# Drawn settings of operand places and product orders behind the last product of an encoder step

## The chip, the cores and the metric

The kernel runs on one core of one Trainium2 chip. The metric is the device time of one execution in microseconds (us). A core has a matrix engine (TensorE, PE in the profile; its weight loads are listed apart, as PEld), VectorE (DVE), ScalarE (ACT), GpSimd (POOL) and SyncE (SP), and 16 DMA engines that are fed by queues. Operands lie in SBUF, an on-chip memory of 128 partitions; TensorE writes its sums to PSUM, which has eight banks of 512 float32 columns in each partition. One product of TensorE takes a block of weights of 128 rows by up to 128 columns from SBUF, streams up to 512 columns of a second operand through it, and adds the result to columns of one bank.

## The reference

The reference is one inference step of a one-layer streaming encoder, for 1024 new prompt frames and 64 frames of a running stream, in float32:

```python
def mixer(xn, conv_prefix, attn_fn, w_in, w_conv, w_conv_out, w_attn_out, w_out):
    proj = xn @ w_in
    ...
    cv, conv_state = causal_conv(cc * ch, conv_prefix, w_conv)
    ya = (cb * cv) @ w_conv_out
    o, new_k, new_v = attn_fn(heads(q), heads(k), heads(v))
    yb = o.reshape(B, L, ATT_DIM) @ w_attn_out
    merged = jax.nn.sigmoid(ga) * ya + jax.nn.sigmoid(gb) * yb
    return merged @ w_out, conv_state, new_k, new_v

def trunk(...):
    m, cs, nk, nv = mixer(rmsnorm(x, g_mix[l]), ...)
    x = x + m
    x = x + (jax.nn.silu(xn2 @ w_ff1) * (xn2 @ w_ff3)) @ w_ff2
    return rmsnorm(x, g_final), ...
```

Here xn2 is rmsnorm(x, g_ffn). Attention reads a band of nine chunks of 64 frames with a bias for each distance. The outputs are the two encoded sequences and the new convolution states and key and value caches.

## The kernel before

All 1088 frames (T) are worked on together. Every float32 operand of a product is split by `split` (lines 119 to 122) into a high and a low part in the type float32r, and a product of two float32 matrices becomes three products of TensorE: high by high, high by low, low by high. Where both sides are large, a product of 2 by 2 blocks is made from seven block products in place of eight; `STEPS` gives their order, and each step has its own weights and its own stream.

The stages follow one another on TensorE: norm, transposes (line 408) and values; the projections of `run` (line 218); the gate projections of `product` (lines 294 to 302) beside attention; the merge; the output projection; transposes (line 1135); the first two feed-forward matrices, again through `run`; and the last one, in the loop from line 1462 on. In each step of `run`, line 238 issues 24 products of 272 columns (HN): four blocks k, by three pairs of high and low, by two halves j of the frames, so that two products in a row have the same weights and write two banks in turn. `product` issues three products in a row to one bank.

In the last stage the transposed hidden frames (ht) are the weights, and the split rows of `w_ff2` stream through as 512 columns (line 1508). These rows lie in seven rings, one for each step, which `ring_of` (lines 1266 to 1270) makes: tiles of 128 partitions by 4352 columns (8 times HT, HT = 544). Ring 1 and ring 2 hold the parts for steps 1 and 2. Columns 3072 to 3583 of ring 1 also take squares that ACT writes when it sums up a row's norm (line 1448). The sums are taken out of PSUM by line 1520 on DVE or line 1518 on ACT. PSUM there has the pool `psD`: tag "A" with two buffers, tag "BD" with four, and the tile ys. Behind the last product follow sums, norms and writes of the output (`half_ended`, lines 1443 to 1459), with writes from the queues of ACT and SP.

The tile framework puts in the waits: a tile that takes over a buffer waits for the last reader of the one before, and a reader waits for the writer of what it reads.

Of the kernel before, what the change touches and what calls it, by code (L numbers as in the profile page):

```python
# [8 lines left out]
F32 = mybir.dt.float32  # L9
# [6 lines left out]
P = 128  # L16
# [17 lines left out]
HN = HT // 2  # L34
# [30 lines left out]
def encoder_kernel(ctx: ExitStack, tc: tile.TileContext, ins, outs):  # L65
# [1396 lines left out]
    for b, ks in enumerate(blocks):  # L1462
        first, final = b == 0, b == len(blocks) - 1
        nk = blocks[b + 1] if not final else []
        for g in range(2):
# [28 lines left out]
            for si, js in turns:  # L1494
# [47 lines left out]
                if final and g == 0 and si == 4:  # L1542
# [9 lines left out]
                    vec.scalar_tensor_tensor(row, row, r[:TS], gfb[:TS], op0=ALU.mult, op1=ALU.mult)  # L1552
                    nc.sync.dma_start(outs["y_sample"], row)

_OUTS = [
    ("y_prompt", (1024, 1024), (1, 1024, 1024)),
    ("y_sample", (64, 1024), (1, 64, 1024)),
# [33 lines left out]
```

## Time and profile before

| what | value |
|---|---|
| median of two runs | 1518.12 us (1518.03 and 1518.2) |
| span of the profiled execution, first to last instruction | 1513.8 us |
| mean granted clock of TensorE in it | 0.994 |
| line 238, products of 272 columns, as its commonest group: mean length of one | 288 ns |
| line 1508, products of 512 columns into A: count and mean length | 528, 393 ns |
| line 903, transposes of attention: count and mean length | 240, 277 ns |

The profile is taken from one execution. Times in its rows are in us from the start of the span. Products of TensorE are pipelined: one is still under way when the next starts, so that the length of one is more than the distance from one start to the next. The chain of waits follows the work that ended last back to the start, and gives for each piece its start and length.

### The profile page before, as it was taken

The page shows a single profiled execution, that of the slowest core. Times are in us where ns is not written, and L with a number is a line of the kernel's source. Part 1 is how long each engine was busy: PE and PEld are TensorE (multiplying, and loading weights), DVE is VectorE, ACT ScalarE, POOL GpSimd, SP SyncE. Part 2 cuts the span into 40 slices and gives each one's busy share as a digit, 9 for nine tenths or more (in the row PEclk, how much of TensorE's full clock was granted, in tenths as well). Part 3 has the DMA queues.
Part 4 walks back from the last instruction along what each step waited for, and adds up shares of the span by engine and source line. Part 5 has one row for each costly group of instructions (what it writes and reads, how often), then busy time and mean ns, then how long its engine had stood idle before and what let it go on. Part 6 is the DMA issues. An engine that isn't in the chain of part 4 may idle for free.

```text
span 1513.8 us, 26451 instructions
## 1 busy us (share of the span) xinstructions
PE 1476.9 (98%) x10178; PEld 1381.1 (91%) x10178; DVE 981.2 (65%) x1843; ACT 682.7 (45%) x1397; POOL 128.7 (9%) x236
## 2 busy tenths in 40 slices
PE   7999999999999999999999999999999999999997
PEld 5799999999999999998889999999999998788886
DVE  6886465642776752763489667666666668857576
ACT  6654433333776752542256444444444445402123
POOL 1210010001111121000100011100001011000000
PEclk9999999999999999999999999999999999999999
DMA  7597524168676529554432434443334449667675
GB/s 233 181 305 245 184 78 135 57 187 234 181 186 176 151 82 293 164 167 145 140 126 77 143 134 152 144 148 120 117 142 157 143 177 317 234 221 235 222 259 202
DMA packets 167518, 264.73 MB, mean 175 GB/s; under 512 B 19008, under 2 KB 103168, under 8 KB 167264
## 3 DMA queue, kind: packets, MB, share of 16 engines
q1 hardware_dynamic: 146736, 198.23, 42.2%
q0 software_dynamic: 19504, 62.71, 11.4%
q10 hardware_dynamic: 1152, 2.10, 0.4%
q8 instruction: 80, 1.31, 0.4%
q14 instruction: 46, 0.38, 0.1%
HBM read 171.06 MB, written 91.92 MB: 174 GB/s over the span
## 4 chain that ended last, share of the span: by engine, by line
PE 79%; DMA 8%; DVE 6%; ACT 3%; issue 3%; SPq 1%; POOL 0%; ACTq 0%; POOLq 0%; DVEq 0%
PE Aa L238 9%; PE Ab L238 9%; PE A L1508 7%; PE Da L238 4%; PE Db L238 4%; PE D L1508 3%; PE Bb L238 2%; PE Ba L238 2%; PE B L1508 2%; PE wo L1066 2%; PE wo L1068 2%; PE wo L1067 2%; PE t L903 2%; PE Ak L238 2%; PE g L300 2%
## 5 line engine op out<-in xcount | busy, mean ns | idle before, releaser
L1508 PE MATMUL A<-ring,ht 128*128 128x512 f32 x528 | 126.6, 393 | 3.6 <-ACT acc L1518 1.9
L1508 PEld LDWEIGHTS A<-ring,ht 128*128 128x128 f32 x528 | 98.8, 188 | 27.2 <-ACT acc L1518 3.2
L300 PE MATMUL g<-xn,whp 128*128 128x272 f32 x384 | 113.2, 295 | 0.0
L301 PE MATMUL g<-xn,whp 128*128 128x272 f32 x384 | 112.0, 292 | 0.0
L302 PE MATMUL g<-xn,wlp 128*128 128x272 f32 x384 | 111.6, 291 | 0.0
L121 ACT CAST ring<-w2r 128x512 fp32r<-128x512 f32 (+1 forms) x78 | 43.4, 587 | 105.7 <-PE A L1508 52.6
L121 ACT CAST hq<-sa 128x512 fp32r<-128x512 f32 x77 | 47.7, 619 | 86.4 <-DVE sa L1239 56.6
L814 DVE CUSTOM_DVE_ANT_0 p<-s,bb 128x640 f32<-128x640 f32 (+5 forms) x72 | 47.5, 661 | 45.5 <-DMA bb<-bias_d 28.6
L1227 POOL DMA_DIRECT2D h_d<-hq x77 | 40.9, 532 | 416.5 <-DVE hq L122 242.1
L122 DVE TENSOR_TENSOR hq<-sa,hq 128x512 fp32r<-128x512 f32 x77 | 53.1, 690 | 33.4 <-ACT hq L121 33.3
L300 PEld LDWEIGHTS g<-xn,whp 128*128 128x128 f32 x384 | 72.6, 189 | 1.0
L302 PEld LDWEIGHTS g<-xn,wlp 128*128 128x128 f32 x384 | 72.6, 189 | 0.5
L301 PEld LDWEIGHTS g<-xn,whp 128*128 128x128 f32 x384 | 72.7, 189 | 0.3
L1508 PE MATMUL D<-ring,ht 128*128 128x512 f32 x264 | 63.9, 393 | 1.3 <-ACT acc L1518 1.3
L122 DVE TENSOR_TENSOR wla<-rawa,wha 128x512 fp32r<-128x512 f32 x56 | 38.5, 687 | 40.5 <-ACT wha L121 40.5
L238 PE MATMUL Aa<-tt,wha 128*128 128x272 f32 x352 | 59.1, 289 | 2.5 <-ACT tt L121 2.5
L1508 PEld LDWEIGHTS D<-ring,ht 128*128 128x128 f32 x264 | 49.5, 188 | 13.1 <-ACT acc L1518 1.8
L122 DVE TENSOR_TENSOR ring<-w2r,ring 128x512 fp32r<-128x512 f32 (+1 forms) x78 | 49.0, 647 | 14.4 <-ACT ring L121 14.2
L238 PE MATMUL Ab<-mg,whb 128*128 128x272 f32 x352 | 58.4, 288 | 0.0
L238 PE MATMUL Aa<-mg,wha 128*128 128x272 f32 x352 | 58.3, 288 | 0.0
L238 PE MATMUL Ab<-tt,whb 128*128 128x272 f32 x352 | 58.2, 287 | 0.0
L121 ACT CAST wha<-rawa 128x512 fp32r<-128x512 f32 x56 | 34.8, 621 | 51.3 <-PE Ab L238 35.3
(519 smaller groups left out, 4368.2 us busy)
## 6 DMA issues: line engine op xcount, KB each, us to landing
h_d<-hq POOLq DMA_DIRECT2D x77, 512.0 KB, 3.5
ht<-h_d SPq DMA_DIRECT2D x154, 256.0 KB, 3.7
rawa<-in_w_ff SPq DMA_DIRECT2D x11, 1024.0 KB, 5.9
rawb<-in_w_ff SPq DMA_DIRECT2D x11, 1024.0 KB, 5.4
w2r<-in_w_ff SPq DMA_DIRECT2D x11, 1024.0 KB, 5.8
qd<-q_d SPq DMA_DIRECT2D x32, 272.0 KB, 4.7
rawp<-in_w_in SPq DMA_DIRECT2D x6, 1024.0 KB, 5.9
u_d<-scr SPq DMA_DIRECT2D x8, 544.0 KB, 4.6
```

The costliest lines, as they stand in the source:

```text
L121: act.copy(hi, src)
L122: vec.tensor_tensor(lo, src, hi.bitcast(F32), op=ALU.subtract)
L238: mm(t[:, j, :HN], w[:, k, :], x[p][:, l, k, j * HN : (j + 1) * HN], start=p in (1, 2, 7) and k == 0 and n == 0, stop=k == 3 and n == 2, s ...
L300: mm(out, a, p, start=k == 0, stop=False)
L301: mm(out, a, q, start=False, stop=False)
L302: mm(out, b, p, start=False, stop=k == kt - 1)
L814: vec.tensor_tensor_reduce(out=s if len(ps.shape) == 2 else s.rearrange("p (a b) -> p a b", a=2), in0=ps, in1=bias if len(ps.shape) == 2 e ...
L903: nc.tensor.transpose(tp[:, i * P : (i + 1) * P], s[:, i * P : (i + 1) * P], ident)
L1066: mm(ps, x(k, 0), wh, start=f, stop=False)
L1067: mm(ps, x(k, 0), wl, start=False, stop=False)
L1227: nc.gpsimd.dma_start(h_d[p, c - 1], hq.rearrange("p i l t -> p (i l t)").bitcast(F32))
L1508: mm(t, ht[k][:, j, x], w[:, l], start=p in (1, 2, 7) and k == 0 and n == 0, stop=k == len(ks) - 1 and n == 2, skip_group_check=p in (6, 5 ...
```

## The change

Behind the last stage a loop is added. It takes ring 1 as the stream, ring 2 as the weights, and two new tiles of PSUM, pr (tag "A") and pq (tag "BD"), which nothing reads. There are 640 settings of 24 products of 272 columns, with the loop of `run`: four blocks k by six combinations of weights w, stream l and half j. Each setting draws the places of its operands. The first 320 keep the order of line 238, the others draw an order of the six. The distance of the two halves is 336 columns, in some of the last 160 settings 320 or 352; the step from one block k to the next is 0, 16 or 32 columns of the stream, and the offsets d, dw and dl are multiples of 8 columns up to 56. Behind them stand 256 transposes of blocks of 128 by 128 from ring 1, taken as float32, into pr.

```diff
+    pr = psD.tile([P, 512], F32, tag="A", name="pr", bufs=2)
+    pq = psD.tile([P, 512], F32, tag="BD", name="pq", bufs=4)
+    mv, st = ring_of(1), ring_of(2)
+    PAIRS = [(0, 0, 0), (0, 0, 1), (0, 1, 0), (0, 1, 1), (1, 0, 0), (1, 0, 1)]
+    draw = random.Random(7)
+    for i in range(640):
+        six = list(PAIRS)
+        if i >= 320:
+            draw.shuffle(six)
+        e = 16 if i < 480 or i % 3 else draw.choice((0, 32))
+        step = draw.choice((0, 0, 16, 32))
+        d, dw, dl = (draw.randrange(0, 64, 8) for _ in range(3))
+        for k in range(4):
+            for w, l, j in six:
+                a = 128 + 2048 * l + dl * l + j * (320 + e) + step * k
+                b = 128 + d + 512 * k + w * (192 + dw)
+                mm(
+                    (pr, pq)[j][:, :HN], st[:, b : b + P], mv[:, a : a + HN],
+                    start=k == 0, stop=k == 3, skip_group_check=True,
+                )
+    wide = mv.bitcast(F32)
+    for i in range(16):
+        for n in range(16):
+            a = 128 + 8 * (i % 8) + 128 * (n % 8) + 64 * (i // 8)
+            nc.tensor.transpose(pr[:, n % 4 * P : n % 4 * P + P], wide[:, a : a + P], ident)
```

More of the change, by code (lines that the diff above doesn't have):

```diff
@@ L1553, in encoder_kernel @@
                     nc.sync.dma_start(outs["y_sample"], row)
+    import random
+    pr = psD.tile([P, 512], F32, tag="A", name="pr", bufs=2)
[23 more added lines that the diff above has]
+            nc.tensor.transpose(pr[:, n % 4 * P : n % 4 * P + P], wide[:, a : a + P], ident)
 _OUTS = [
```

## The prediction

> **What bounds the kernel now.** I read the page first: the busy shares (columns: busy us, share of the span, instructions) and the row of granted clock.
>
> ```profile
> span 1513.8 us, 26451 instructions
> PE 1476.9 (98%) x10178; PEld 1381.1 (91%) x10178; DVE 981.2 (65%) x1843; ACT 682.7 (45%) x1397; POOL 128.7 (9%) x236
> PEclk9999999999999999999999999999999999999999
> q8 instruction: 80, 1.31, 0.4%
> ```
>
> TensorE is busy 98% of the span, and there is one weight load for each product (10178 and 10178), so no product saves its load even where two in a row use the same weights. The clock stays at 9 tenths or more in all 40 slices. As the work is added to TensorE, behind its last product, what matters is how far apart products of 272 columns start when nothing holds them up. A product's own duration (288 ns in the groups) is no help, because products overlap. So next comes the chain of waits, in its middle (columns: start, length in us, what): from 36 consecutive rows of line 238, all of 24 products, the first, the last, and one of each other length that occurs.
>
> ```profile
> 1153.60 3.00 PE Da L238 x24
> 1156.60 3.01 PE Aa L238 x24
> ...
> 1168.61 2.99 PE Db L238 x24
> ...
> 1258.50 3.00 PE Db L238 x24
> ```
>
> From the start of the first row to the start of the last lie 35 rows, 840 products, and 104.90 us: 124.9 ns a product. No row is shorter than 2.99 or longer than 3.01 us, which is 0.4 ns a product either way. The table of stretches says whether that stretch is undisturbed (columns: stretch, us, then busy time and count for PE, PEld, DVE, ACT, POOL, then clock, DMA share, GB/s):
>
> ```profile
> 1000.00:1250.00 250.00, 250.00 (x2004) 250.00 (x2003) 166.75 (x280) 110.81 (x210) 25.59 (x48) 1.00 0.41 147
> 1505.80:1513.80 8.00, 0.04 (x1) 0.00 (x0) 3.43 (x11) 2.48 (x7) 0.00 (x0) 0.75 0.38 142
> ```
>
> In 250 us TensorE is never idle, at full clock; the 2004 products, of which some two were already running at the start, confirm 125 ns. The second row is the end of the kernel: from 1505.8 on TensorE has no work, and 8 us go to the last sums, norms and output writes on DVE, ACT and the queues. What bounds the span is therefore TensorE up to 1505.8 and a chain of small DVE and ACT steps after it.
>
> **The change part by part.** Where it starts: the timeline of the end (start, length, engine, line, what, count).
>
> ```profile
> 1501.80 0.69 DVE L1520 TENSOR_TENSOR acc<-A,acc 128x512 f32<-128x512 f32 x1
> 1504.78 1.07 PE L1508 MATMUL A<-ring,ht 128*128 128x512 f32 x4
> 1505.98 0.68 DVE L1520 TENSOR_TENSOR acc<-A,acc 128x512 f32<-128x512 f32 x1
> 1506.75 0.63 ACT L1448 ACTIVATE ring<-acc 128x512 fp32r<-128x512 f32 x1 [0.46 <-DVE n2y L157]
> 1509.01 0.75 DVE L1458 SCALAR_TENSOR_TENSOR acc<-acc,n4y,gfb 128x512 f32<-128x512 f32 x1
> 1509.76 0.37 ACTq L1457 DMA_DIRECT2D out_y_prompt<-acc  x1
> ```
>
> The last product ends at 1504.78 + 1.07 = 1505.85. Four products in 1.07 us, of which one lasts about 0.39, start (1.07 - 0.39) / 3 = 0.23 us apart, so the next could start at 1505.85 - 0.39 + 0.23 = 1505.69. The new tile pr takes the older of the two buffers of tag A; its last reader is the DVE sum at 1501.80, done by 1502.49. If it got the other one, it would wait for the sum at 1505.98 to 1506.66, 1.0 us. Buffers of tag BD were read earlier still. The moving operand lies in ring 1, into whose columns 3072 to 3583 ACT writes squares until 1507.38; the change reads columns below 2952. If the order were kept for the whole tile, the start would slip to 1507.4, by 1.7 us. I take no wait, and 0 to 2 us for the range. The norms and output writes of the tail don't depend on the new work; they end at about 1513.8 and are covered by it.
>
> The products: 640 settings of 24 make 15,360. Each has 128 x 128 weights and 272 columns, the form of line 238, so 15,360 x 124.88 ns = 1918.2 us, all of it on TensorE and on the path that sets the end. Half of the settings have line 238's own order; the other half are shuffled within each group of six. The nearest row to another order is in the gated projections, where three products in a row go to one bank in the order high, high, low. Of its rows the first of one run and the first behind it, 12 products apart:
>
> ```profile
> 606.78 0.29 PE L300 MATMUL ya<-u,whp 128*128 128x272 f32 x1
> ...
> 608.29 0.67 PE L300 MATMUL yb<-ob,whp 128*128 128x272 f32 x4
> ```
>
> 1.51 us / 12 = 125.8 ns. On the 7,680 shuffled products the 0.9 ns more would be 7 us; that is the upper end of the order's price, and 0 the lower. I take 0, because line 238 has the same two banks in turn and is the row that the new products resemble most.
>
> The transposes: 256, each of 128 columns with the data as weights and the identity streaming, as lines 408 and 1135 issue them, eight in a row. A row of each line at full clock, one at half clock, its clock from the stretch that holds it, and the length of one:
>
> ```profile
> 757.43 1.04 PE L1135 MATMUL xt<-ident,xg 128*128 128x128 f32 x8
> ...
> 54.48 1.06 PE L408 MATMUL xt<-ident,scr 128*128 128x128 f32 x8 [1.71 <-DVE scr L393]
> ...
> 56.81 1.91 PE L408 MATMUL xt<-ident,scr 128*128 128x128 f32 x8
> ...
> 56.00:58.00 2.00, 1.19 (x6) 1.37 (x7) 0.50 0.60 166
> ...
> L1135 PE MATMUL xt<-ident,xg x72: 222/273/300, 753.9 to 807.0; 128*128 128x128 f32 x64, 64*128 64x64 f32 x8
> ```
>
> Eight in 1.04 us, the last of 0.27, start 0.77 / 7 = 0.110 us apart; 256 make 28.1 us. At half clock the eight take 1.91 us, about 0.11 us more for each. [...] I take full clock, for the nearest rows with no gap before them show it.
>
> Instruction code: the instruction queue of the page moved 80 packets, 1.31 MB, which fits the 2 x 10178 instructions of TensorE (16 KB for 256 of them). The 31,232 new ones need 122 packets more. In the undisturbed 250 us above some 4000 instructions, 16 packets, were consumed at the same pace without a gap, so I cost it at nothing. The two loads of DVE and ACT that ran beside the products then are absent in the added part; nothing here can make it slower.
>
> The sum, against the profiled execution: 1505.7 + 1918.2 + 28.1 + 0.2 for the end of the last transpose = 3452.2. Behind it stands the closing of the program. From the last output write's issue (1509.76) to the end (1513.8) are 4.0 us, a write's flight among them, which the new end hasn't; so 0 to 4, taken as 2. Span 3454. The median of the runs is 1518.12, 4.3 us over the span; with the same 4.3 the time is **3458 us**, 2.28 times the time before.
>
> **The rivals.**
>
> *Places cost something of their own.* The change draws offsets between weights and stream in steps of 8 columns, which line 238 doesn't vary. That a place matters at all shows in the last stage, in the chain of waits:
>
> ```profile
> 1480.99 4.08 PE B L1508 x18
> 1485.07 4.20 PE A L1508 x18
> ```
>
> The same shape, 18 products of 512 columns, takes 226.7 ns each in one and 233.3 in the other, with other places and other banks: 2.9%. For it: this row. Against it: the rows of line 238 lie between 2.99 and 3.01 us although they read seven streams and many weight buffers at different places. If the drawn places were all the bad ones, 2.9% of 1918 is 56 us: 3514. If line 238 now has the middle, the drawn ones lie within half of that on either side: 3430 to 3486. Chance 0.10 for more than 3471, 0.07 for less than 3450.
>
> *The clock falls in the transposes.* In place of 110 ns each takes up to 0.11 us more, 256 x 0.11 = 28 us: 3486, less what passes before the gate closes. For it: line 408 ran at half clock in this very trace. Against it: that was 2 us behind an idle gap of 1.71 us, and the row of line 1135 ran at full clock. Chance 0.16. [...]
>
> *The products are not run.* Nothing reads pr or pq. Were work without a reader dropped on the way to the chip, nothing would be added: 1518 us, no change. It would decide from the point where less than 30 us, about 240 products, is left. For it: in the profile of before every product has a reader, so the case isn't tested. Against it: nothing in the profile shows that anything was dropped. Chance 0.02.
>
> *Late code.* If the 122 packets came late by half a microsecond each, it would be 61 us, 3519; no gap in 250 us speaks for it. Chance 0.03.
>
> **How the numbers follow.** The forecast (3458; its own range is 3450 to 3471: 6 us down and up for 0.4 ns a product, 2 down for the closing, 7 up for the order) has 0.62. The range reaches to half the spread of the 512-column rows below, 3430, and to the whole of it above, 3515, which takes in the clock; outside are the dropped products, late code, and a small part of the two cases of places, about 1 in 10. A measurement of this kernel tells 2%, 30 us, from no change. All cases but the dropped work are slower by over 100%: slower 0.98, within 2% 0.015, and 0.005 for faster, for which I see no mechanism.
>
> **What would show it.** In the profile of the changed kernel: a group of x15360 products of 272 columns at the line of the new loop, and x256 transposes; TensorE without idle time from 1505.7 on; 24 products in 3.00 us in every slice; PEclk 9 up to the last slice, or 5 in the last if the transposes lose the clock; about 202 packets on the instruction queue; the output writes ending near 1513. It is wrong if the settings differ by more than a few tenths of a nanosecond a product, if the shuffled half is slower than the first, or if TensorE shows gaps.

## The result and the profile after

The changed kernel took 3463.49 us (median of two runs, 3462.35 and 3464.64) against 1518.12 us: a ratio of 2.2819, with a 95% interval of 2.2753 to 2.2885. The forecast was 3458 us.

The page of the changed kernel, in the rows that answer to those of before:

```profile
span 3462.5 us, 57683 instructions
PE 3429.8 (99%) x25794; PEld 3334.5 (96%) x25794; DVE 981.7 (28%) x1843; ACT 683.3 (20%) x1397; POOL 128.9 (4%) x236
PEclk9999999999999999999999999999999999999999
q8 instruction: 202, 3.31, 0.4%
L1573 PE MATMUL pr<-ring,ring 128*128 128x272 f32 x7680 | 1768.4, 288 | 0.0
L1573 PE MATMUL pq<-ring,ring 128*128 128x272 f32 x7680 | 1768.2, 288 | 0.0
```

DVE, ACT and POOL did what they did before; TensorE has 15,616 products more, each with its load, and no idle time in front of any of them (the 0.0 of the two groups). The granted clock stayed at 9 tenths or more in all 40 slices, and 122 packets of code more were fetched (202 against 80).

The ends of the added work, from the timeline of TensorE (start, length, what, count), and below them two rows of ACT and one of DVE from the same stretch:

```profile
1505.08 2.20 PE L1508 MATMUL A<-ring,ht 128*128 128x512 f32 x9
1507.12 0.29 PE L1573 MATMUL pr<-ring,ring 128*128 128x272 f32 x1
...
3433.46 28.11 PE L1581 MATMUL pr<-ident,ring 128*128 128x128 f32 x256
...
1506.53 0.63 ACT L1448 ACTIVATE ring<-acc 128x512 fp32r<-128x512 f32 x1 [1.23 <-DVE acc L1520]
1507.42 0.68 DVE L1520 TENSOR_TENSOR acc<-A,acc 128x512 f32<-128x512 f32 x1
1508.19 0.63 ACT L1448 ACTIVATE ring<-acc 128x512 fp32r<-128x512 f32 x1 [0.45 <-DVE n2y L157]
```

The last product of before ends at 1507.28, and the first new one starts 0.16 us ahead of that end: no wait for a buffer or for ring 1. It starts before the last sum from tag A (1507.42 us), so pr had the older buffer, and the new products run on while ACT writes squares into ring 1 until 1508.82 us. From 1507.12 to 3433.46 are 1926.34 us for 15,360 products, 125.41 ns each. The 256 transposes took 28.11 us, and the program closed 0.93 us behind them, at 3462.5.

The stretches say where the 125.41 ns come from. The first row lies in the settings with line 238's order, the second and third in the shuffled ones; the columns are those of the prediction's table of stretches:

```profile
1510.00:1910.00 400.00, 400.00 (x3192) 400.00 (x3191) 1.13 (x3) 0.73 (x1) 0.00 (x0) 1.00 0.01 4
...
2470.00:2870.00 400.00, 400.00 (x3192) 400.00 (x3191) 0.00 (x0) 0.00 (x0) 0.00 (x0) 1.00 0.00 1
2870.00:3430.00 560.00, 560.00 (x4465) 560.00 (x4464) 0.00 (x0) 0.00 (x0) 0.00 (x0) 1.00 0.00 1
```

Some two products of each count were under way when the stretch began; 400 us over 3190 are 125.4 ns, shuffled or not. From the starts of all products, the first 320 settings have a mean of 125.37 ns and the last 320 one of 125.46. Single settings, each the mean of its 24 products, lie between 123.6 and 127.0 ns, with a standard deviation of 0.55.

### The profile page after: what moved, and what is told of

Its sections match the earlier page's. It is cut to its first block, busy times and chain, and to the rows that moved or that the text cites. A ratio compares the mean times of both kernels' runs of the same rounds, so it can differ in the third digit from the quotient of the medians.

```text
span 3462.5 us, 57683 instructions
## 1 busy us (share of the span) xinstructions
PE 3429.8 (99%) x25794; PEld 3334.5 (96%) x25794; DVE 981.7 (28%) x1843; ACT 683.3 (20%) x1397; POOL 128.9 (4%) x236
## 4 chain that ended last, share of the span: by engine, by line
PE 75%; issue 19%; DMA 2%; POOL 2%; DVE 1%; ACT 1%; POOLq 0%; SPq 0%; ACTq 0%; DVEq 0%
PE pr L1573 28%; PE pq L1573 28%; PE A L1508 3%; PE D L1508 2%; POOL h_d L1227 1%; PE g L300 1%; PE g L302 1%; PE g L301 1%; PE pr L1581 1%; PE B L1508 1%; PE t L903 1%; PE Ak L238 1%; PE pv L928 1%; PE Acc L238 1%; PE Ach L238 1%
## 5 line engine op out<-in xcount | busy, mean ns | idle before, releaser
L1573 PE MATMUL pr<-ring,ring 128*128 128x272 f32 x7680 | 1768.4, 288 | 0.0
L1573 PE MATMUL pq<-ring,ring 128*128 128x272 f32 x7680 | 1768.2, 288 | 0.0
L1573 PEld LDWEIGHTS pr<-ring,ring 128*128 128x128 f32 x7680 | 1345.2, 188 | 0.0
L1573 PEld LDWEIGHTS pq<-ring,ring 128*128 128x128 f32 x7680 | 1344.9, 188 | 0.0
L1508 PE MATMUL A<-ring,ht 128*128 128x512 f32 x528 | 126.6, 393 | 3.6 <-ACT acc L1518 1.9
L814 DVE CUSTOM_DVE_ANT_0 p<-s,bb 128x640 f32<-128x640 f32 (+5 forms) x72 | 47.5, 661 | 43.1 <-DMA qd<-q_d 28.1
L238 PE MATMUL Ab<-tt,whb 128*128 128x272 f32 x352 | 58.2, 287 | 0.0
```

Of the source, the lines that this page charges most:

```text
L238: mm(t[:, j, :HN], w[:, k, :], x[p][:, l, k, j * HN : (j + 1) * HN], start=p in (1, 2, 7) and k == 0 and n == 0, stop=k == 3 and n == 2, s ...
L814: vec.tensor_tensor_reduce(out=s if len(ps.shape) == 2 else s.rearrange("p (a b) -> p a b", a=2), in0=ps, in1=bias if len(ps.shape) == 2 e ...
L1508: mm(t, ht[k][:, j, x], w[:, l], start=p in (1, 2, 7) and k == 0 and n == 0, stop=k == len(ks) - 1 and n == 2, skip_group_check=p in (6, 5 ...
L1573: mm((pr, pq)[j][:, :HN], st[:, b : b + P], mv[:, a : a + HN], start=k == 0, stop=k == 3, skip_group_check=True,)
```

## The experiments

Two questions were left by the result: why a product took 125.41 ns and not the 124.88 of line 238, and whether the spread of the settings belongs to their places. Theory one: the places decide, and line 238 has a mixture of them that is a little cheaper than the drawn one. Its rivals: something else in the loop (the order, the banks), or the spread is scatter of the records. Two further experiments take up the rivals of the prediction that the clock falls in transposes and that places weigh more with 512 columns. All cadences below are distances from one start to the next in the trace.

**The strides of line 238.**

```diff
-        if i >= 320:
-            draw.shuffle(six)
...
-                a = 128 + 2048 * l + dl * l + j * (320 + e) + step * k
-                b = 128 + d + 512 * k + w * (192 + dw)
+                a = 2176 * l + 544 * k + 272 * j
+                b = 2048 * w + 128 * k
```

> The 15,360 added products read with the strides of line 238 (stream 2176 for the low part, 544 for k, 272 for the half; weights 128 apart for k, 2048 between high and low), in its order, with nothing drawn. If the drawn places make the products dearer, the cadence falls from 125.4 to the 124.9 ns of line 238, 8 us less than the changed kernel: 3455 us. If it is something else that the loop has and line 238 has not, it stays at 125.4 ns, 3463 us.

```profile
1510.00:3420.00 1910.00, 1910.00 (x15249) 1910.00 (x15248) 0.00 (x0) 0.00 (x0) 0.00 (x0) 1.00 0.00 1
```

1910 us over 15,247 are 125.27 ns; the time was 3460.27 us, a ratio of 2.2865 (2.2825 to 2.2904). That is between the two expectations: 0.14 of the 0.53 ns went with the strides and the order. The strides alone are not the place, though: no trace here shows how far line 238's streams lie from their weight buffers, and it need not be the distance of ring 1 from ring 2. The profiled execution took 4.9 us less than the changed kernel's, but 3.5 of them are the part in front, as the added work began at 1503.65 us here.

These strides also reach columns 3072 to 3583 of ring 1, which the drawn places leave out, and here TensorE did wait for the squares of line 1448:

```profile
1504.72 0.63 ACT L1448 ACTIVATE ring<-acc 128x512 fp32r<-128x512 f32 x1 [0.46 <-DVE n2y L157]
1505.50 0.65 PE L1571 MATMUL pq<-ring,ring 128*128 128x272 f32 x3 [0.31 <-ACT ring L1448]
```

So the order is kept by columns, as the prediction took it, and not for the whole tile.

**One setting, 640 times.**

```diff
-        if i >= 320:
-            draw.shuffle(six)
-        e = 16 if i < 480 or i % 3 else draw.choice((0, 32))
-        step = draw.choice((0, 0, 16, 32))
-        d, dw, dl = (draw.randrange(0, 64, 8) for _ in range(3))
+        e, step, d, dw, dl = 16, 16, 24, 40, 8
```

> All 640 settings have the same places (e 16, step 16, d 24, dw 40, dl 8) and the same order. If places set the cost of a setting, all 640 means agree within 0.1 ns, at one value between 123.6 and 127.0 ns, the extremes of the drawn ones (time 3436 to 3488 us). If the spread of the drawn settings is scatter of the records, the means spread by the same 3.5 ns and the mean is 125.4 ns, 3463 us.

The stretch from 1510 to 3420 us, as for the kernel above:

```profile
1510.00:3420.00 1910.00, 1910.00 (x15215) 1910.00 (x15214) 0.91 (x2) 0.73 (x1) 0.00 (x0) 1.00 0.01 2
```

125.55 ns, and 3464.92 us (ratio 2.2894, 2.2847 to 2.2940). The settings no longer spread: but for the last (125.8, with the step to the transposes in it), all means lie between 125.54 and 125.58 ns. So the spread of the changed kernel is no scatter. Within a setting the 24 distances from start to start repeat in each of them to a rounding, from 122.5 ns at one position to 131.7 at another.

**The changed kernel again**, with no edit:

> The changed kernel once more. If a setting's cost is fixed by its places and order, the 640 means of this run agree with those of the first to about 0.05 ns each (correlation near 1) and their mean is 125.4 ns again; if they are scatter, the correlation is near 0. Time 3456 to 3467 us.

It took 3459.98 us (3456.52 to 3463.98 in four runs; ratio 2.2843, 2.2758 to 2.2929). The mean of the 640 settings was 125.41 ns again, and the means of the two executions have a correlation of 0.999, with 0.04 ns as the largest difference. So what a setting of this loop cost was fixed by its places and its order. What differs between executions is the part in front: the added work began at 1503.60 us here, and at 1507.12 in the first profile.

**One pair of operands in each setting**, to find what in the places decides:

```diff
...
+        block, s = divmod(i, 160)
+        a = 128 + (0, 8, 8, 0)[block] * s
+        b = 128 + (8, 0, 8, 1)[block] * s
+        for k in range(24):
+            mm(
+                (pr, pq)[i % 2][:, :HN], st[:, b : b + P], mv[:, a : a + HN],
...
```

> Each of the 640 settings is now 24 products with one and the same pair of operands, to one bank; the transposes are left out. In four blocks of 160 settings move: the weights by 8 columns a setting, the stream by 8 columns, both by 8 columns, the weights by one column. If the cost comes from weights and stream meeting in one part of SBUF, their distance decides: the first two blocks vary by some ns with a period, the third is flat. If each operand's own place decides, the third block varies as well. If only the mixture of places within a setting counts, all blocks are flat to 0.1 ns. Time about 3430 us in all cases, plus or minus 25.

The timeline of TensorE in the first block, where the weights move by 32 bytes from row to row:

```profile
1558.52 3.12 PE L1565 MATMUL pq<-ring,ring 128*128 128x272 f32 x24
1561.48 3.20 PE L1565 MATMUL pr<-ring,ring 128*128 128x272 f32 x24
1564.51 3.20 PE L1565 MATMUL pq<-ring,ring 128*128 128x272 f32 x24
1567.55 3.20 PE L1565 MATMUL pr<-ring,ring 128*128 128x272 f32 x24
1570.59 3.18 PE L1565 MATMUL pq<-ring,ring 128*128 128x272 f32 x24
1573.60 3.17 PE L1565 MATMUL pr<-ring,ring 128*128 128x272 f32 x24
1576.61 3.17 PE L1565 MATMUL pq<-ring,ring 128*128 128x272 f32 x24
1579.62 3.13 PE L1565 MATMUL pr<-ring,ring 128*128 128x272 f32 x24
1582.58 3.12 PE L1565 MATMUL pq<-ring,ring 128*128 128x272 f32 x24
```

The lengths come round after eight rows, 256 bytes: 3.12, three of 3.20, 3.18, 3.17, 3.17, 3.13, and 3.12 again. In distances from start to start that is 123.2 ns in the cheapest place and 126.7 in the dearest. When the stream moves instead, the range is the same (123.4 to 126.8 ns), with a period of 16 rows: 13 of the 16 places cost what their distance cost in the first block, to 0.4 ns, and three are off by 0.8 to 1.7 ns. When both move together, all settings lie between 125.1 and 125.5 ns:

```profile
2600.07 3.17 PE L1565 MATMUL pq<-ring,ring 128*128 128x272 f32 x24
2603.08 3.17 PE L1565 MATMUL pr<-ring,ring 128*128 128x272 f32 x24
2606.08 3.17 PE L1565 MATMUL pq<-ring,ring 128*128 128x272 f32 x24
```

So in this run, with one pair repeated, the distance of the weights from the stream decided, for the most part modulo 256 bytes; the three places show that it isn't quite all. Steps of one column (4 bytes) brought values from 123.2 to 129.0 ns. Here 24 products in a row write one bank, at a mean of 125.4 and 125.5 ns in the first two blocks, so a single bank was not dear as such.

**Chosen distances**, with 24 different pairs in a setting as in a real loop:

```diff
...
+                p = n % 2
+                u = (0, 0, 32 * p, 32 * p)[block]
+                v = (24, 40, 24 + 32 * p, 56 - 32 * p)[block]
+                a = 128 + 1408 * l + 384 * j + 128 * k + u
+                b = 128 + 512 * k + 256 * w + v
...
```

> Four blocks of 160 settings in line 238's order, with 24 different pairs of places in each; the transposes are left out. In the first two blocks every distance of weights from stream is 96 or 160 bytes (modulo 256), where one repeated pair cost 123.2 and 126.7 ns. In the third a product's own weights lie 96 and the next product's 224 bytes from its stream (125.6 ns there), in the fourth it is the other way round. If the next weights, loaded while the stream runs, are what counts: 123.2, 126.7, 125.6, 123.2 ns. If a product's own weights count: 123.2, 126.7, 123.2, 125.6. If the pattern belongs to repeated pairs alone: about 125.4 in all four. Time about 3426 us.

A stretch of each block:

```profile
1510.00:1975.00 465.00, 465.00 (x3772) 465.00 (x3772) 0.33 (x1) 0.31 (x1) 0.00 (x0) 1.00 0.01 3
1985.00:2455.00 470.00, 470.00 (x3753) 470.00 (x3751) 0.00 (x0) 0.00 (x0) 0.00 (x0) 1.00 0.00 1
2465.00:2945.00 480.00, 480.00 (x3791) 480.00 (x3791) 0.00 (x0) 0.00 (x0) 0.00 (x0) 1.00 0.00 1
2950.00:3415.00 465.00, 465.00 (x3773) 465.00 (x3772) 0.00 (x0) 0.00 (x0) 0.00 (x0) 1.00 0.00 1
```

With two products less in each count: 123.3, 125.3, 126.7 and 123.3 ns. The third and fourth blocks tell the two readings apart. With the own weights at the cheap distance and the next ones elsewhere the block is dear; the other way round it is as cheap as the first. Of the two it is the distance of the next product's weights that fits; their load starts with this product (in the changed kernel, a load for pq and the product into pr before it both at 3427.28 us). The sizes agree only in part: the second block was expected at 126.7 and the third at 125.6 ns. Even in the first block, with one distance throughout, the products alternate between 125.8 and 120.8 ns.

The drawn settings go further. Both executions of the changed kernel have a start for each of the 15,360 products, and the distances follow from the draws. Single products repeat their cost from one execution to the other (correlation 0.98). Sorted by the distance of the next weights modulo 256 bytes, though, the eight classes have means of 125.1 to 125.8 ns, and account for 1% of the variance (the mean square of the spread); the class of 96 bytes, the cheapest for one pair, has 125.5. The products' own weights account for less. So the distance priced the loop that repeats it (123.2 to 126.7 ns), and not a product in the drawn loop; what sets the cost there stays open.

**Sizes.** The loop is that of the one pair, with the weights moving by 8 columns a setting, and with m of 128, 64, 32 and 128 columns of weights and c of 272, 272, 272 and 512 columns of stream in its four blocks:

```diff
...
+        b = 128 + 8 * s
+        for k in range(24):
+            mm(
+                (pr, pq)[i % 2][:m, :c], st[:, b : b + m], mv[:, 128 : 128 + c],
...
```

> Four blocks of 128 settings, each 24 products with one repeated pair; the weights move by 8 columns a setting; the transposes are left out. Weights of 128, 64 and 32 columns with a stream of 272, then 128 with 512. If the distance counts because the load of the weights and the stream meet in one part of SBUF, the swing of 3.4 ns of the first block shrinks with the load, to about 1.7 and 0.9 ns, and stays about 3.4 ns (1.5%) with 512 columns. If it counts by the two start places alone, the swing is 3.4 ns in the first three. If it goes with the stream's length, it is about 6.5 ns with 512 columns, the 226.7 to 233.3 ns of the last stage. Time about 1504 + 9216 x 0.1254 + 3072 x 0.232 = 3374 us.

Without the first and the last setting of each block, the swing was 123.2 to 126.7 ns with 128 columns of weights, 123.3 to 126.6 with 64, 122.4 to 124.9 with 32, and 227.0 to 233.7 with 512 columns of stream. Rows of the last block:

```profile
2737.23 5.76 PE L1566 MATMUL pq<-ring,ring 128*128 128x512 f32 x24
2742.82 5.61 PE L1566 MATMUL pr<-ring,ring 128*128 128x512 f32 x24
2748.27 5.75 PE L1566 MATMUL pq<-ring,ring 128*128 128x512 f32 x24
```

A row that starts 5.45 us before the next (2742.82 to 2748.27) has 227.1 ns a product, its neighbour with 5.59 us has 232.9. The swing went with the length of the stream (6.7 ns for 512 columns, 3.4 for 272) and fell far less than the columns of weights: to 2.5 ns, three quarters, for a quarter of them. The expectation for a meeting of the load with the stream in SBUF was 0.9 ns there. So such a meeting isn't shown, and where the swing comes from stays open.

**The drawn settings with 512 columns**, 320 of them:

```diff
-    for i in range(640):
+    for i in range(320):
...
-        if i >= 320:
+        if i >= 160:
...
-                    (pr, pq)[j][:, :HN], st[:, b : b + P], mv[:, a : a + HN],
+                    (pr, pq)[j], st[:, b : b + P], mv[:, a : a + 512],
```

> 320 settings in place of 640, each product with 512 columns in place of 272. If the difference of 226.7 and 233.3 ns between lines of the last stage comes from the places, the settings spread over at least that range and the mean lies near 230 ns: 7680 x 230 = 1766 us, about 3304 us. If it comes from something else there (the stage's banks or its loads of ht), all settings cost the same, at 226.7 ns or less: 3279 us or less.

It took 3314.97 us, with 231.9 ns a product and settings between 229.2 and 233.9. The mixture of distances spread over 4.7 ns, against 6.7 for the single pair, and its mean lies above the middle of the last stage's two values (226.7 and 233.3). Places alone can give that whole range, as the experiment before showed (227.0 to 233.7 ns); the stage's banks aren't needed for it. That the stage's two values do come from its places isn't shown.

**Columns and weights.** 27 blocks of 256 products in place of the settings:

```diff
+    sizes = [(n, m) for m in (128, 64, 32) for n in (64, 128, 192, 256, 272, 320, 384, 448, 512)]
+    for i, (n, m) in enumerate(sizes):
+        for k in range(256):
+            a, b = 128 + 8 * (k % 64), 128 + 128 * (k % 16)
+            mm(
+                (pr, pq)[i % 2][:m, :n], st[:, b : b + m], mv[:, a : a + n],
...
```

> In place of the settings 27 blocks of 256 products: 64 to 512 columns, with weights of 128, 64 and 32 columns; the transposes are left out. From 125.4 ns at 272 and 231.9 ns at 512 columns a straight line gives 0.444 ns a column and 4.7 ns a product. If the line is the stream's own rate, the size of the weights changes nothing and the added stretch takes 911 us, time about 2420 us. If loading the weights beside the stream takes the time above half of the half-clock cadence (226.7 / 2 = 113.3 ns at 272 columns), weights of 32 columns bring 272 columns to about 116 ns and 128 columns of weights set a floor under the short products.

It took 2500 us, 80 more than the straight line. The added stretch was 90 us longer than the line's 911, as the part in front ended some 8 us earlier. Stretches of the blocks of 128 columns with weights of 128, of 272 columns with 128, of 128 with 64, of 272 with 32, and of 512 with 32:

```profile
1550.00:1600.00 50.00, 50.00 (x236) 50.00 (x236) 0.00 (x0) 0.00 (x0) 0.00 (x0) 0.50 0.00 1
...
1665.00:1690.00 25.00, 25.00 (x203) 25.00 (x202) 0.00 (x0) 0.00 (x0) 0.00 (x0) 1.00 0.01 1
...
1905.00:1917.00 12.00, 12.00 (x204) 12.00 (x203) 0.00 (x0) 0.00 (x0) 0.00 (x0) 1.00 0.01 3
...
2275.00:2300.00 25.00, 25.00 (x204) 21.79 (x202) 0.00 (x0) 0.00 (x0) 0.00 (x0) 1.00 0.01 1
2440.00:2490.00 50.00, 50.00 (x219) 23.43 (x218) 0.00 (x0) 0.00 (x0) 0.00 (x0) 1.00 0.00 1
```

272 columns cost 124.8 ns with weights of 128, 125.0 with 64 and 124.2 with 32: a quarter of the load changed the cost by 0.6 ns. At half clock line 238 has 226.7 ns a product (12 products from 112.94 to 115.66 us of the changed kernel, clock 0.50); what a product costs at full clock above half of that, 113.3 ns, was still there with weights of 32 columns (124.2 ns), so it wasn't the load. With weights of 32 columns the cadence runs from 59.8 ns at 128 columns to 230.8 at 512 in a straight line of 0.445 ns a column and 2.8 ns a product. Of the 90 us, 81 are the first two blocks, 64 and 128 columns behind weights of 128: the first row stands at a clock of 0.50, with 213 ns a product. Another 8 are the block of 192 columns: it began at half clock too, and at full clock it cost 111.6 ns, against 88.3 behind weights of 64.

**Transposes alone.**

```diff
-    for i in range(640):
+    for i in range(0):
-    for i in range(16):
+    for i in range(256):
...
-            a = 128 + 8 * (i % 8) + 128 * (n % 8) + 64 * (i // 8)
+            a = 128 + 8 * (i % 8) + 128 * (n % 8) + 64 * (i // 8 % 2)
```

> The added products are left out and 4096 transposes are made in place of 256. If transposes keep the clock open, each costs 109 ns: 447 us, and the time is about 1957 us at a clock of 1.0. [...]

```profile
1510.00:1940.00 430.00, 430.00 (x3942) 430.00 (x3941) 0.00 (x0) 0.00 (x0) 0.00 (x0) 1.00 0.01 2
```

1955.11 us: 109.2 ns a transpose at full clock, through 447 us of nothing else. The clock was open when they began, so this shows that they kept it open, at 1.00, not that they would open a closed one.

**Short products**, to see which streams let the clock fall: 2048 of 128 columns, then 2048 of 64.

```diff
+    for n in (128, 64):
+        for k in range(2048):
+            a, b = 128 + 8 * (k % 64), 128 + 128 * (k % 16)
+            mm(
+                (pr, pq)[n // 64 - 1][:, :n], st[:, b : b + P], mv[:, a : a + n],
...
```

> The settings and transposes are left out; behind the last product come 2048 products of 128 columns, then 2048 of 64, all with weights of 128 columns. If the load of 128 columns and the stream follow one another, 128 columns take 109 ns like the transposes, and 64 columns about as long or less. If the gate closes on what TensorE streams, it stays open for the first (as for the transposes) and closes for the second, 213 ns: 1504 + 224 + 436 = about 2165 us. If it stays open for both: about 1950 us. If it closes for both: about 2380 us.

```profile
1510.00:1730.00 220.00, 220.00 (x1972) 220.00 (x1972) 0.00 (x0) 0.00 (x0) 0.00 (x0) 1.00 0.01 2
1740.00:2160.00 420.00, 420.00 (x1971) 420.00 (x1970) 0.00 (x0) 0.00 (x0) 0.00 (x0) 0.50 0.00 1
```

111.6 ns and an open clock for 128 columns; 64 columns fell to half clock 2 us after they began and stayed there, at 213 ns. The time was 2171 us.

## Why the prediction was right, step by step

The time lay 5.5 us above the forecast, inside its own range of 3450 to 3471. Against the profiled execution, whose time was 3464.64 us, the terms stand like this:

| term | predicted | profile after |
|---|---|---|
| start of the added work | 1505.69 | 1507.12 |
| 15,360 products | 1918.2 (124.88 ns) | 1926.3 (125.41 ns) |
| 256 transposes, with the end of the last | 28.3 | 28.1 |
| closing | 2 | 0.9 |
| time above the span | 4.3 | 2.1 |

- **Start.** No wait was there, as argued from the ring's columns and the tags; line 238's strides, which do reach the squares' columns, had one. The 1.4 us are the kernel in front: its last nine products began at 1503.64 us in the profile before, at 1505.08 in this one, and between 1494.3 and 1504.9 in those of the experiments.
- **Products.** The mechanism held: products one behind the other, none waiting, the cadence of line 238. The size was off by 0.53 ns a product, 8 us, the largest error of the sum. The prediction took line 238's mixture of places as a fair one. The second run of the changed kernel repeated every setting's cost, and one setting alone gave 125.55, line 238's strides on the two rings 125.27 ns: each mixture has its own mean. How line 238 comes to 124.88 stays open. By the prediction's own sign, settings that differ by more than a few tenths of a nanosecond, its picture of one cadence for all settings was wrong: they lie up to 3.4 ns apart, 2.97 to 3.05 us for 24 products and not 3.00 in every slice. The time came out because the mean of 640 drawn settings fell 0.4% from line 238; the prediction took that over from line 238's rows, which show nothing of the drawn places, so part of the hit is luck.
- **Order.** Taken at nothing, with 7 us as the upper end. The shuffled half was dearer by 0.09 ns, 0.7 us on 7,680 products. The halves also have different draws, and with 0.55 ns from setting to setting two draws of 320 differ by some 0.04 ns, and easily by twice that, anyway, so a price of the order isn't shown; no run changed the order alone. The 125.8 ns of the gated projections were one stretch of 12 products: over 1760 distances of these projections without a gap (below 160 ns, in the profile before) the mean is 125.3.
- **Transposes.** Right to 0.2 us. The rival that the clock falls had 0.16 and is out: the 256 ran at 1.00, and 4096 of them, float32 and of 128 columns, kept an open clock open (1.00 from 1510 to 1940 us); whether they would open a closed one no run here shows.
- **Places.** The rival was right that places cost something of their own, and its row, 18 products in 4.08 or 4.20 us, had a swing of the true size (227.0 to 233.7 ns with one pair). Its bounds of 2.9% on the sum were too wide: 640 draws average the places out, and their mean of 125.41 ns is that of one pair over all distances (125.4 and 125.5).
- **Code and dropped work.** 202 packets were fetched, as counted, and no gap was seen; all 15,616 products ran.
- **Above the span.** 4.3 us were the median of other executions minus the span of the profiled one. With each execution's own span beside its time, as after, it is 2.1. The two small terms at the end, 3.3 us too much together, hid part of the products' error; that is luck too.

## What to carry to other kernels

A stream of equal products is priced by the distance from one start to the next in an undisturbed stretch, over some hundred of them, and not by the length of one; that gave 1.95 ms to within 8 us. Here the price was a mean over operand places, and for a loop that repeats one pair it was up to 1.5% off either way (123.2 to 126.7 and 227.0 to 233.7 ns), so where such a loop matters, move its weights by 32 bytes and measure again. A span is to be compared with the time of its own execution.

## What the runs showed of the hardware

- With one pair of operands repeated, a product's cost went with how far the weights lay from the stream, for the most part modulo 256 bytes: 123.2 to 126.7 ns for 272 columns, 227.0 to 233.7 for 512. In the drawn loop the cost of a product recurred (correlation 0.98 between two executions), but this distance accounted for 1% of its variance.
- The size of the weights counted for short streams and hardly for one of 272 columns: 272 columns took 124.2 to 125.0 ns behind weights of 128, 64 or 32 columns; 128 and 192 columns both took 111.6 ns behind weights of 128 columns, against 59.8 for 128 columns behind 32 and 88.3 for 192 behind 64.
- The granted clock fell to 0.50 without any idle time in the records, on products of 64 columns behind weights of 128 (213 ns). It stayed at 1.00 on 128 columns behind weights of 128, as a product (111.6 ns) or as a transpose (109.2). Products of 64 columns behind weights of 64 took 58.2 ns, and the 128 columns that came behind those stood at 1.00. In the run with columns and weights, 128 columns that came behind those of 64, both with weights of 128, stayed at half clock for all of their 55 us, though the same stream kept an open clock open for 229 us in the run of short products; 192 columns behind them ran at 213 ns for 5.4 us and at 111.6 from then on.
